# State-space stage: running sums spread over the partitions by DMA through DRAM in place of selector products, and C.B read from PSUM

## Chip, cores and metric

The kernel runs on one core of one Trainium2 chip. The time is device time of one execution, in microseconds (us); the runs shown are compared by their median. A profile is one further execution, seen by the hardware profiler. "Page" below is the page that the profile makes of that execution.

## What is computed

Two transformer-like blocks in a row, in float32, on 512 tokens of 1024 features. The first block holds a state-space mixer (Mamba-2) and a sliding-window attention; the second one a differential attention, a sparse attention and two convolutional feed-forward layers. The change concerns the state-space mixer alone. Cut to what matters there (32 heads of 64 features in 8 groups of 4 heads, chunks of 128 tokens, 4 chunks):

```python
a_cs = jnp.cumsum(a, axis=-1)                        # a = dt * A; within a chunk, per head
seg = a_cs[..., :, None] - a_cs[..., None, :]
decay = jnp.exp(jnp.where(causal, seg, -jnp.inf))
cb = jnp.einsum('bclgn,bcsgn->bcgls', Cc, Bc)
y_diag = jnp.einsum('bcgrls,bcsgrp->bclgrp', cb[:, :, :, None] * decay, x)
...
y_off = jnp.einsum('bclgn,bcgrpn,bcgrl->bclgrp', Cc, h_in, jnp.exp(a_cs))
return (y_diag + y_off).reshape(b, L, SSM_HEADS, P)
```

So each head needs its running sum a_cs twice: as a difference between any two tokens of a chunk (the decay), and exponentiated per token (for what comes in from earlier chunks).

## The kernel before

Everything is kept as features on partitions by tokens along the free dimension. Products of weights with activations are exact to float32 by splitting both into a high and a low part (wH, wL, hH, hL): three TensorE products of 128 by 128 by 512 for each block of 128 weights rows, 24 for one output block, all recorded under line 365 (`gemm`). The weights come as a stream: a load of 512 KB (raw, four buffers) on SP's queue, a copy on ScalarE that makes wH (L319), a subtraction on VectorE that makes wL (L321); wH and wL have four buffers each. One such chunk feeds the 24 products of one output block.

The stage (`mamba`) computes the time steps and the running sums first. `pacs` holds the sums with tokens on partitions, `acs` (L616 to L618) holds them with heads on rows 0 to 31 and, as a rest that a float32r copy leaves, on rows 32 to 63. Then it loops over the 8 groups. For a group g:

- Four projections (two x blocks, B, C), each followed by a short convolution on VectorE (u, L626; xc, L631) and Silu on ScalarE (L633); two more projections for the gate z (L638, L639).
- Transposes of x (ps_t, L650) make xdt and xde on VectorE; transposes of B (L661) make bt on ScalarE (L662).
- C.B of the four chunks goes to a PSUM bank (L666) and is copied by ScalarE to cbs (L669).
- The states h after each chunk (L674, L679 to L682).
- For each pair of heads (i = 0, 1): for each head r a product selr x acs (L692) sets the head's running sums on all 128 partitions of a bank pa; four Relu on ScalarE (L696, one per chunk, with pacs as bias) and an Exp (L698) make the decay m; GpSimd masks it (L699); VectorE multiplies it with cbs (L701). Eight products yd of m with xdt follow (L705). A product sel2 x acs (L711) does the same for the pair's exponentials e (L714). Three products yf of the states with C (L716). VectorE puts them together into y (L720 to L724).

ps_s, the PSUM banks of yd, yf and pa, has 2 buffers, ps_t 2, ps_g (projections) 3, ps_o 1.

The code names no order between engines: a scheduler in the building layer puts each engine's instructions in a row, and so lets the projection products of group g + 1 run among the small products at the end of group g. Each engine, and SP's DMA queue, runs its row in order. After groups 3 and 5 a part of the output product is done (L735 to L740).

Of the kernel before, what the change touches and what calls it, by code (L numbers as in the profile page):

```python
# [9 lines left out]
F32 = mybir.dt.float32  # L10
F32R = mybir.dt.float32r
# [3 lines left out]
ALU = mybir.AluOpType  # L15

P = 128
# [21 lines left out]
W3 = 0  # L39
ALL_STAGES = ("mamba", "swa", "da", "ffn0", "dsa", "ffn1", "final")  # L40
# [5 lines left out]
# ---------------------------------------------------------------- host layout  # L46
# [17 lines left out]
def _stage_blocks(stage, a):  # L64
    """The stage's weights as [128, 128] blocks in the order in which the program takes them."""
# [148 lines left out]
# ---------------------------------------------------------------- the program  # L214
class _Kernel:
    """The stages, all on features by tokens: x is the residual stream, hH + hL the normed operand without its
    1 / rms (exactly, as two float32r parts), rb and rt 1 / rms on all partitions and per token."""
# [24 lines left out]
    # ---- shared state  # L242
# [60 lines left out]
    # ---- the weight stream  # L303
# [5 lines left out]
    def wchunk(self, pool=None, name=""):  # L309
        """Emits the next group of 8 blocks: load, high and low parts."""  # L310
# [14 lines left out]
    def wget(self, n=1):  # L325
        """High and low parts of the stream's next n blocks."""
        c, r = divmod(self.wi, 8)
        assert r + n <= 8
        if r == 0:
            while self.wemit <= min(c + 1, self.ws.shape[0] - 1):  # L330
                self.wchunk()
            self.wchunks.pop(c - 6, None)
        H, L = self.wchunks[c]
        self.wi += n
        return H[:, r * P:(r + n) * P], L[:, r * P:(r + n) * P]
# [4 lines left out]
    # ---- PSUM and products of features by tokens  # L340
# [9 lines left out]
    def gemm(self, w, H, L, cuts, M=P, spread=False, late=False):  # L350
        """The product, cut by tokens: (PSUM view, first token, tokens). spread takes score banks as well; late
        leaves what needs L to the end."""
# [19 lines left out]
    # ---- norms  # L372
    def square_in(self, src, k, c0, cn, eng=None, acc=None):
        """acc += src ** 2."""
# [9 lines left out]
    def parts_of_x(self, k, g, t0, t1, T):  # L384
        """High and low parts of x * g of feature block k, tokens t0 to t1 of the residual."""
# [13 lines left out]
    def next_h(self, k, g, t0, t1, T):  # L399
        """What the next layer takes of feature block k."""  # L400
# [4 lines left out]
    def rsqrt(self, dst, v, rows=P):  # L405
        """dst = v ** -0.5 of small SBUF operands: a power, then a Newton step."""
# [17 lines left out]
    def token_sums(self, T, half=None, acc=None):  # L424
        """Sums of acc over the features, a column per token tile."""
# [11 lines left out]
    def spread_rows(self, src, T, half=None):  # L437
        """PSUM views [128, tokens] with src[t] of a token-on-partition column set on all partitions."""
# [16 lines left out]
    def norm_end(self, T, half=None):  # L455
        """rt and rb of the tokens from acc."""
# [8 lines left out]
    def post_stats(self, half, acc, rg=None):  # L465
        """PSUM view with 1 / rms of (rg * ys) on all partitions, for half of the first block's tokens; acc holds
        the squares of ys."""
# [18 lines left out]
    def post_update(self, half, rp, ys, xs, g_post, g_next, T_next):  # L486
        """x = xs + g_post * rp * ys, and the next layer's operand."""
# [24 lines left out]
    def out_halves(self, pool, H, L, ys, xs, g_post, g_next, T_next, acc, rg=None, part=True):  # L512
        """The last part of a first-block layer's output product, half of the tokens at a time, and the norm; ys
        holds what comes before if part."""
        nc = self.nc
        n = len(H)
        # all of the weights stay for the second half: the first ones in the ring, the others in the pool
# [28 lines left out]
    # ---- the state-space mixer  # L546
    def mamba(self, g_next):
        nc, T = self.nc, SEQ
        tc = self.tc
        with ExitStack() as ctx:  # L550
# [7 lines left out]
            selr = cp.tile([64, 32], F32R, name="selr")  # L558
            nc.vector.tensor_tensor(selr, self.ident[:64, :32], self.ident[:64, 32:64], ALU.add)
# [3 lines left out]
            # time steps, 128 tokens x (4 chunks x 32 heads)  # L563
# [29 lines left out]
            # decays  # L593
# [22 lines left out]
            acs = cp.tile([64, T], F32R, name="acs")  # L616
            nc.scalar.activation(acs[:32], ps[:32, :T], AF.Copy)
            nc.vector.tensor_tensor(acs[32:64], ps[:32, :T], acs[:32].bitcast(F32), ALU.subtract)  # L618

            for g in range(GROUPS):  # L620
                xc, sz = [], []
                for i, b in enumerate((2 * g, 2 * g + 1, 16 + g, 24 + g)):
# [19 lines left out]
                # tokens on partitions: x * dt, x * dt * decay to the chunk's end, B  # L642
# [20 lines left out]
                # C B per chunk, keys on partitions  # L663
                cb = self.ps("t")
# [3 lines left out]
                cbs = wp.tile([P, T], F32, name="cbs", bufs=1)  # L668
                nc.scalar.activation(cbs, cb[:, :T], AF.Copy)  # L669
                # states after each chunk  # L670
# [13 lines left out]
                # outputs, two heads (a block of features) at a time  # L684
                for i in range(2):
                    yd = self.ps("s")
                    yf = self.ps("s")
                    ms = []
                    for r in range(2):
                        hd = 4 * g + 2 * i + r  # L690
                        pa = self.ps("s")
                        nc.tensor.matmul(pa[:, :T], selr[:, hd:hd + 1].to_broadcast([64, P]), acs, start=True,  # L692
                                         stop=True)
                        m = wp.tile([P, T], F32, name="m", bufs=2)
                        for c in range(4):
                            nc.scalar.activation(m[:, P * c:P * c + P], pa[:, P * c:P * c + P], AF.Relu,  # L696
                                                 bias=pacs[:, 32 * c + hd:32 * c + hd + 1], scale=-1.0)
# [763 lines left out]
```

## Time and profile before

| | |
|---|---|
| median of 3 runs | 2216.05 us (2211.14 to 2216.69) |
| span of the profiled execution | 2209.3 us; its own time is not given apart from the span, which is 6.75 us under the median of the runs |
| instructions | 38252 |
| TensorE busy, share of span | 2141.4 us, 97% |
| VectorE busy | 1542.3 us, 70% |
| ScalarE busy | 1001.8 us, 45% |
| GpSimd busy | 252.1 us, 11% |
| DMA, mean over the span | 79 GB/s |
| the state-space stage's loop | about 45 to 440 us |

How to read it: PE is TensorE's products, PEld its weight loads (which run beside products), DVE VectorE, ACT ScalarE, POOL GpSimd, SPq the DMA queue of SyncE. "L365" is a line of the kernel. An arrow such as ps_g<-hH,wH names the tile written and the tiles read. Products are pipelined, so a product's listed duration is longer than the distance between two starts. In a list of waits, "A <- B" says that A's engine stood idle until B was done.

### The profile page before, as it was taken

To read this page: it belongs to the slowest core of one execution; us is meant where nothing else is said; L and a number is where in the kernel's file an instruction comes from. 1 tells how busy PE (TensorE), PEld (TensorE's weight loads), DVE (VectorE), ACT (ScalarE), POOL (GpSimd) and SP (SyncE) were. 2 spreads that over 40 slices of the span, in tenths; PEclk is the share of its full clock that TensorE was granted. 3 is DMA by queue.
4 is the path that set the end of the run, shared out by engine and by line. 5 is a ranking of instruction groups with operands and counts; after the bars stand their busy time and mean duration, and the time that the engine had idled before them with its cause. 6 is when DMAs were issued, how large, how long until landed. Compare 5 with 4: busy or idle time off the path is not lost.

```text
span 2209.3 us, 38252 instructions
## 1 busy us (share of the span) xinstructions
PE 2141.4 (97%) x15108; PEld 1908.7 (86%) x15108; DVE 1542.3 (70%) x3336; ACT 1001.8 (45%) x1939; POOL 252.1 (11%) x380
## 2 busy tenths in 40 slices
PE   8999999999998999999999999999999999999998
PEld 6777777787777888888999999979788889999997
DVE  7776676778766677886664466489888866645653
ACT  6565544545775454454342243343444434423431
POOL 0111010142102211212000000110110110000001
PEclk9999999999999999999999999999999999999999
DMA  5222222233221212222232322321321223323321
GB/s 182 67 58 77 76 77 77 70 107 96 58 67 57 89 58 51 76 68 67 77 96 86 96 87 86 90 65 58 87 59 49 69 77 87 95 87 96 96 86 48
DMA packets 52306, 174.49 MB, mean 79 GB/s; under 512 B 7328, under 2 KB 9376, under 8 KB 52128
## 3 DMA queue, kind: packets, MB, share of 16 engines
q1 hardware_dynamic: 50976, 171.01, 26.2%
q8 instruction: 119, 1.95, 0.4%
q10 hardware_dynamic: 1152, 1.05, 0.1%
q14 instruction: 59, 0.48, 0.1%
HBM read 160.23 MB, written 2.10 MB: 73 GB/s over the span
## 4 chain that ended last, share of the span: by engine, by line
PE 54%; DVE 9%; issue 2%; ACT 1%; POOL 1%; POOLq 0%; DVEq 0%; ACTq 0%
PE ps_g L365 29%; PE ps_s L365 13%; PE ps_o L1243 2%; PE ps_s L1007 2%; PE ps_o L1133 2%; PE ps_g L790 1%; DVE wL L321 1%; DVE sel L1345 1%; PE ps_t L1035 1%; DVE m L1344 1%; PE ps_s L972 1%; POOL rs_r L411 1%; PE ps_t L1032 1%; DVE sel L1325 1%; DVE hL L396 1%
## 5 line engine op out<-in xcount | busy, mean ns | idle before, releaser
L365 PE MATMUL ps_g<-hH,wL 128*128 128x256 f32 (+3 forms) x1912 | 614.0, 321 | 0.4 <-DVE wL L321 0.4
L365 PE MATMUL ps_g<-hL,wH 128*128 128x256 f32 (+3 forms) x1912 | 609.7, 320 | 2.7 <-DVE hL L396 2.7
L365 PE MATMUL ps_g<-hH,wH 128*128 128x256 f32 (+3 forms) x1912 | 608.2, 318 | 0.4 <-ACT hH L391 0.3
L319 ACT ACTIVATE wH<-raw 128x1024 fp32r<-128x1024 f32 x294 | 310.8, 1058 | 396.4 <-PE ps_g L365 228.4
L321 DVE TENSOR_TENSOR wL<-raw,wH 128x1024 fp32r<-128x1024 f32 x294 | 364.3, 1241 | 146.2 <-ACT wH L319 145.8
L365 PEld LDWEIGHTS ps_g<-hH,wH 128*128 128x128 f32 x1912 | 362.2, 189 | 28.5 <-issue 4.5
L365 PEld LDWEIGHTS ps_g<-hL,wH 128*128 128x128 f32 x1912 | 361.4, 189 | 29.3 <-DVE hL L396 4.3
L365 PEld LDWEIGHTS ps_g<-hH,wL 128*128 128x128 f32 x1912 | 362.4, 190 | 26.9 <-issue 5.5
L365 PE MATMUL ps_s<-hH,wH 128*128 128x256 f32 (+5 forms) x608 | 178.3, 294 | 7.9 <-ACT hH L391 7.9
L365 PE MATMUL ps_s<-hH,wL 128*128 128x256 f32 (+5 forms) x608 | 178.2, 293 | 0.6 <-DVE wL L321 0.6
L365 PE MATMUL ps_s<-hL,wH 128*128 128x256 f32 (+5 forms) x608 | 177.2, 294 | 0.8 <-DVE hL L396 0.4
L382 POOL TENSOR_TENSOR acc<-acc,sq 128x512 f32<-128x512 f32 (+3 forms) x62 | 75.5, 1217 | 554.5 <-ACT sq L381 552.9
L1380 DVE SCALAR_TENSOR_TENSOR c<-u,prm,c 128x528 f32<-128x528 f32 (+1 forms) x176 | 132.9, 755 | 3.5 <-ACT c L1377 1.8
L772 POOL TENSOR_TENSOR rt<-rt,S 128x272 f32<-128x272 f32 (+3 forms) x80 | 81.1, 1016 | 414.9 <-DVE rt L770 325.5
L365 PEld LDWEIGHTS ps_s<-hH,wH 128*128 128x128 f32 (+2 forms) x608 | 115.6, 190 | 10.2 <-ACT hH L391 9.0
L365 PEld LDWEIGHTS ps_s<-hL,wH 128*128 128x128 f32 (+2 forms) x608 | 114.6, 189 | 5.0 <-DVE hL L396 3.7
L365 PEld LDWEIGHTS ps_s<-hH,wL 128*128 128x128 f32 (+2 forms) x608 | 116.0, 191 | 3.3 <-DVE wL L321 1.4
L365 PE MATMUL ps_g<-aH,wH 128*128 128x256 f32 (+1 forms) x418 | 118.1, 283 | 0.3
L365 PE MATMUL ps_g<-aL,wH 128*128 128x256 f32 (+1 forms) x418 | 118.1, 282 | 0.0
L365 PE MATMUL ps_g<-aH,wL 128*128 128x256 f32 (+1 forms) x418 | 118.1, 282 | 0.0
L797 ACT ACTIVATE aH<-sg 128x528 fp32r<-128x528 f32 (+1 forms) x44 | 28.1, 639 | 126.8 <-DVE sg L1385 126.8
L365 PE MATMUL ps_s<-aH,wH 128*128 128x256 f32 (+1 forms) x286 | 80.4, 281 | 0.4 <-ACT aH L797 0.4
(498 smaller groups left out, 4556.1 us busy)
## 6 DMA issues: line engine op xcount, KB each, us to landing
raw<-in_ws_dram SPq DMA_DIRECT2D x294, 512.0 KB, 3.6
k<-k SPq DMA_DIRECT2D x32, 264.0 KB, 3.6
x<-in_xT_dram SPq DMA_DIRECT2D x8, 256.0 KB, 4.8
xo<-in_xT_dram SPq DMA_DIRECT2D x8, 256.0 KB, 5.4
k<-k SPq DMA_DIRECT2D x4, 256.0 KB, 7.5
out_dram<-x SPq DMA_DIRECT2D x8, 128.0 KB, 1.7
out_dram<-x ACTq DMA_DIRECT2D x8, 128.0 KB, 1.7
C<-in_tab_dram SPq DMA_DIRECT2D x2, 264.0 KB, 5.1
```

The costliest lines, as they stand in the source:

```text
L319: nc.scalar.activation(H, self.raw, AF.Copy)
L321: nc.vector.tensor_tensor(L, self.raw, H.bitcast(F32), ALU.subtract)
L365: nc.tensor.matmul(ps[:M, :cn], w[k][a][:, :M], b[k][:, c0:c0 + cn], start=i == 0, stop=i == 3 * n - 1)
L382: (eng or nc.gpsimd).tensor_tensor(acc, acc, s[:, :cn], ALU.add)
L396: self.nc.vector.scalar_tensor_tensor(L, self.x[k][:, t0:t1], self.col(g, k), H.bitcast(F32), ALU.mult, ALU.subtract)
L411: nc.gpsimd.tensor_tensor(r, v, self.mhalf[:rows, :n], ALU.pow)
L772: nc.gpsimd.tensor_tensor(t, t, S[:, cc], ALU.mult)
L797: nc.scalar.activation(H[:, cols], src, AF.Copy)
L1007: nc.tensor.matmul(ps, q[:, r, t0 - q0:e - q0], k[:, r, k0:k1], start=n == 0, stop=n == 1 and not last)
L1133: nc.tensor.matmul(dst, aT[j], vs[j][:ENDS[j] - STARTS[j], hc], start=j == 0, stop=j == i)
L1243: nc.tensor.matmul(dst, vs[j][:ENDS[j] - STARTS[j], hc], pT[r][j], start=j == 0, stop=j == i, skip_group_check=True)
L1380: nc.vector.scalar_tensor_tensor(c[:, lo:], u[:, t + lo:t + T2], self.col(fw, 3 * b + t), c[:, lo:], ALU.mult, ALU.add)
```

## The change

The running sums are no longer split in two and multiplied with selectors. `acs` stays float32 on 32 partitions and is stored in a DRAM tile (`acs_d`); its exponential is made once for all heads and stored as well (`eas_d`). A function `decay(hd)` loads one head's row of `acs_d` with a DMA that repeats the row on 128 partitions into a tile m (6 buffers), and does Relu, Exp and mask in place; it is called for the four heads at the head of the group's loop. e is loaded in the same way from `eas_d`, two halves of 64 partitions. C.B goes to the bank ps_o instead of ps_t, and VectorE's product of m reads it there; the copy cbs is gone, and the four products of a group stand right behind C.B.

```diff
+MB = 6
...
-            selr = cp.tile([64, 32], F32R, name="selr")
-            nc.vector.tensor_tensor(selr, self.ident[:64, :32], self.ident[:64, 32:64], ALU.add)
+            dram = self.pool(ctx, "md", 1, space=bass.MemoryType.DRAM)
...
-            acs = cp.tile([64, T], F32R, name="acs")
-            nc.scalar.activation(acs[:32], ps[:32, :T], AF.Copy)
-            nc.vector.tensor_tensor(acs[32:64], ps[:32, :T], acs[:32].bitcast(F32), ALU.subtract)
+            acs = wp.tile([32, T], F32, name="acs", bufs=1)
+            nc.scalar.activation(acs, ps[:32, :T], AF.Copy)
+            acs_d = dram.tile([32, T], F32, name="acs_d")
+            nc.sync.dma_start(acs_d, acs)
+            eas = wp.tile([32, T], F32, name="eas", bufs=1)
+            nc.scalar.activation(eas, ps[:32, :T], AF.Exp)
+            eas_d = dram.tile([32, T], F32, name="eas_d")
+            nc.sync.dma_start(eas_d, eas)
+
+            def decay(hd):
+
+                m = wp.tile([P, T], F32, name="m", bufs=MB)
+                nc.sync.dma_start(m, acs_d[hd:hd + 1, :].to_broadcast([P, T]))
+                for c in range(4):
+                    nc.scalar.activation(m[:, P * c:P * c + P], m[:, P * c:P * c + P], AF.Relu,
+                                         bias=pacs[:, 32 * c + hd:32 * c + hd + 1], scale=-1.0)
+                nc.scalar.activation(m, m, AF.Exp, scale=-1.0)
+                nc.gpsimd.affine_select(m, m, pattern=[[0, 4], [1, P]], compare_op=ALU.is_ge, fill=0.0,
+                                        base=0, channel_multiplier=-1)
+                return m
...
+                ms = [decay(4 * g + r) for r in range(4)]
...
-                cb = self.ps("t")
+                cb = self.ps("o")
...
-                cbs = wp.tile([P, T], F32, name="cbs", bufs=1)
-                nc.scalar.activation(cbs, cb[:, :T], AF.Copy)
-                # states after each chunk
+                for m in ms:
+                    nc.vector.tensor_tensor(m, m, cb[:, :T], ALU.mult)
...
-                    ms = []
-                    for r in range(2):
-                        hd = 4 * g + 2 * i + r
-                        pa = self.ps("s")
-                        nc.tensor.matmul(pa[:, :T], selr[:, hd:hd + 1].to_broadcast([64, P]), acs, start=True,
-                                         stop=True)
...
-                        nc.vector.tensor_tensor(m, m, cbs, ALU.mult)
-                        ms.append(m)
...
-                                             ms[r][:, P * c:P * c + P], start=True, stop=True)
+                                             ms[2 * i + r][:, P * c:P * c + P], start=True, stop=True)
...
-                    pa = self.ps("s")
-                    sel2 = wp.tile([64, 2, 64], F32R, name="sel2")
-                    nc.vector.tensor_copy(sel2, selr.bitcast(F32)[:, hd:hd + 2, None].to_broadcast([64, 2, 64]))
-                    nc.tensor.matmul(pa[:, :3 * P], sel2.rearrange("k a b -> k (a b)"), acs[:, P:], start=True,
-                                     stop=True)
                     e = wp.tile([P, 3 * P], F32, name="e")
-                    nc.scalar.activation(e, pa[:, :3 * P], AF.Exp)
+                    for r in range(2):
+                        nc.sync.dma_start(e[64 * r:64 * r + 64],
+                                          eas_d[hd + r:hd + r + 1, P:].to_broadcast([64, 3 * P]))
```

Lines after the change stand one further down up to the stage (L365 becomes L366) and some twenty further down inside it. The scheduler's rows move at three places.

TensorE at the end of group 2 (the third group), before: the rows from the first pair's yf (h is the state) to the second pair's selector products. Rows of L365 are the projection of group 3.

```order
L365 MATMUL ps_g<-hH_85,wL 128x512
L716 MATMUL ps_s<-xc_1184,h_1289 128x128
L716 MATMUL ps_s<-xc_1184,h_1293 128x128
L716 MATMUL ps_s<-xc_1184,h_1298 128x128
L365 MATMUL ps_g<-hL_93,wH 128x512
L705 MATMUL ps_s<-m,xdt 64x128 x7
L692 MATMUL ps_s<-acs,selr 128x512
L365 MATMUL ps_g<-hH_86,wH 128x512
L365 MATMUL ps_g<-hH_86,wL 128x512
L365 MATMUL ps_g<-hL_94,wH 128x512
L365 MATMUL ps_g<-hH_87,wH 128x512
L692 MATMUL ps_s<-acs,selr 128x512
```

The same engine and group after, from the state sums (L693) over the first pair's yd to the second pair's:

```order
L693 MATMUL ps_t<-xde,bt 128x256 x2
L709 MATMUL ps_s<-m,xdt 64x128
L366 MATMUL ps_g<-hL_90,wH 128x512
L709 MATMUL ps_s<-m,xdt 64x128 x7
L366 MATMUL ps_g<-hH_83,wH 128x512
L366 MATMUL ps_g<-hH_83,wL 128x512
L366 MATMUL ps_g<-hL_91,wH 128x512
L366 MATMUL ps_g<-hH_84,wH 128x512
L693 MATMUL ps_t<-xde,bt 128x256
L717 MATMUL ps_s<-xc_1197,h_1304 128x128
L709 MATMUL ps_s<-m,xdt 64x128 x8
```

The second pair's yd moved up to the first state product, eight in a row; the selector products are gone; and in the whole row of a group other products break into the projection eight times, where they did so eleven times.

ScalarE at the end of group 2, before: from the first Relu of m to the second pair's.

```order
L696 ACTIVATE m<-ps_s,pacs 128x128 x5
L662 ACTIVATE bt<-ps_t 128x384
L698 ACT_TABLE_LOAD
L698 ACTIVATE m<-m 128x512
L669 ACTIVATE cbs<-ps_t 128x512
L696 ACTIVATE m<-ps_s,pacs 128x128 x3
L698 ACTIVATE m<-m 128x512
L714 ACTIVATE e<-ps_s 128x384
L696 ACTIVATE m<-ps_s,pacs 128x128 x4
L698 ACTIVATE m<-m 128x512
```

After, at the same place; m here belongs to group 3, sq and yH to group 2, xc_1438 to group 3:

```order
L681 ACTIVATE bt<-ps_t 128x384
L631 ACTIVATE m<-m,pacs 128x128 x5
L633 ACT_TABLE_LOAD
L633 ACTIVATE m<-m 128x512
L631 ACTIVATE m<-m,pacs 128x128 x4
L633 ACTIVATE m<-m 128x512
L382 ACTIVATE sq<-y 128x512
L730 ACTIVATE yH<-y,prm 128x512
L647 ACTIVATE xc_1438<-u,prm 128x512
L320 ACTIVATE wH<-raw 128x1024
L631 ACTIVATE m<-m,pacs 128x128 x4
L633 ACTIVATE m<-m 128x512
```

The decay of a group moved into the end of the group before it, and bt stands ahead of it. In the first group all four m stand ahead of bt, with z's Silu between the third and the fourth.

SP's queue before is one row of 65 raw loads through the stage; after, in groups 2 to 4, it reads:

```order
L307 DMA raw<-in_ws_dram 128x1024 x4
L629 DMA m<-acs_d 128x512 x3
L307 DMA raw<-in_ws_dram 128x1024
L629 DMA m<-acs_d 128x512
L714 DMA e<-eas_d 64x384 x4
L307 DMA raw<-in_ws_dram 128x1024 x5
L629 DMA m<-acs_d 128x512 x3
```

The loads of m and e came in between the weight loads, and every raw load behind one of them leaves after it.

## Rows read from the trace of the kernel before

**Rows 1.** Stretches: us, busy of each engine (instructions), clock, DMA share, GB/s.

```profile
45.00:440.00 395.00, 390.97 (x1898) 300.31 (x1897) 285.04 (x400) 215.63 (x378) 45.76 (x75) 1.00 0.25 74
...
143.47:188.42 44.95, 44.50 (x221) 34.14 (x220) 34.56 (x49) 26.04 (x46) 5.84 (x10) 1.00 0.24 72
```

**Rows 2.** Waits, 45 to 440 us: who for whom, us in total, times, longest.

```profile
ACT wH L319 <- PE ps_g L365: 50.2, 25, 5.1
...
PEld ps_s L705 <- DVE m L701: 9.0, 20, 0.7
...
PE ps_s L705 <- DVE m L701: 4.0, 14, 0.6
```

**Rows 3.** Waits of SP's DMA queue, 40 to 460 us.

```profile
SPq L306 <- DVE wL L321: 388.1, 57, 18.2
```

**Rows 4.** Timeline of TensorE in group 2: start us, us, instruction, count.

```profile
144.44 0.72 PE L692 MATMUL ps_s<-acs,selr 64*128 64x512 f32 x2
145.09 0.51 PE L365 MATMUL ps_g<-hH,wH 128*128 128x512 f32 x1
...
151.20 0.43 PE L711 MATMUL ps_s<-acs,sel 64*128 64x384 f32 x1
151.56 0.50 PE L365 MATMUL ps_g<-hL,wH 128*128 128x512 f32 x1
...
153.35 1.09 PE L705 MATMUL ps_s<-m,xdt 128*64 128x128 f32 x14
154.37 0.50 PE L692 MATMUL ps_s<-acs,selr 64*128 64x512 f32 x1
154.80 0.50 PE L365 MATMUL ps_g<-hH,wH 128*128 128x512 f32 x1
...
155.60 0.39 PE L365 MATMUL ps_g<-hH,wH 128*128 128x512 f32 x1
155.91 0.50 PE L692 MATMUL ps_s<-acs,selr 64*128 64x512 f32 x1
...
156.68 0.39 PE L365 MATMUL ps_g<-hL,wH 128*128 128x512 f32 x1
156.91 0.39 PE L365 MATMUL ps_g<-hH,wH 128*128 128x512 f32 x1
```

**Rows 5.** Groups by line and shape, 45 to 440 us: busy us, mean ns.

```profile
L701 DVE TENSOR_TENSOR m<-m,cbs 128x512 f32<-128x512 f32 x32 | 24.6, 769 | 5.6 <-POOL m L699 5.6
...
L638 DVE TENSOR_TENSOR z<-ps_g,rb 128x512 f32<-128x512 f32 x16 | 11.1, 691 | 31.8 <-PE ps_g L365 31.8
...
L714 ACT ACTIVATE e<-ps_s 128x384 f32<-128x384 f32 x16 | 7.9, 492 | 8.5 <-PE ps_s L711 8.4
```

**Rows 6.** DMA issues of the whole span: count, KB each, median us to landing.

```profile
raw<-in_ws_dram SPq DMA_DIRECT2D x294, 512.0 KB, 3.6
...
out_dram<-x SPq DMA_DIRECT2D x8, 128.0 KB, 1.7
...
posi<-in_pos_dram SPq DMA_DIRECT2D x1, 256.0 KB, 5.3
```

**Rows 7.** Timeline of ScalarE in the first group.

```profile
44.26 0.59 ACT L617 ACTIVATE acs<-ps_t 32x512 fp32r<-32x512 f32 x1
...
54.00 1.06 ACT L319 ACTIVATE wH<-raw 128x1024 fp32r<-128x1024 f32 x1 [3.04 <-PE ps_g L365]
...
55.49 1.38 ACT L696 ACTIVATE m<-ps_s,pacs 128x128 f32<-128x128 f32 x5
56.94 0.49 ACT L662 ACTIVATE bt<-ps_t 128x384 f32<-128x384 f32 x1
57.45 1.28 ACT L698 ACT_TABLE_LOAD   x1
58.74 0.63 ACT L698 ACTIVATE m<-m 128x512 f32<-128x512 f32 x1
```

**Rows 8.** Timeline of VectorE in the first group.

```profile
47.15 1.22 DVE L321 TENSOR_TENSOR wL<-raw,wH 128x1024 fp32r<-128x1024 f32 x1
```

More of the change, by code (lines that the diff above doesn't have):

```diff
@@ L687, in mamba @@
                     yf = self.ps("s")
-                    ms = []
-                    for r in range(2):
-                        hd = 4 * g + 2 * i + r
-                        pa = self.ps("s")
-                        nc.tensor.matmul(pa[:, :T], selr[:, hd:hd + 1].to_broadcast([64, P]), acs, start=True,
-                                         stop=True)
[L694 to L697, printed above, removed]
-                        nc.scalar.activation(m, m, AF.Exp, scale=-1.0)
-                        nc.gpsimd.affine_select(m, m, pattern=[[0, 4], [1, P]], compare_op=ALU.is_ge, fill=0.0,
-                                                base=0, channel_multiplier=-1)
-                        nc.vector.tensor_tensor(m, m, cbs, ALU.mult)
-                        ms.append(m)
                     for c in range(4):
```

## Prediction

> **What bounds the kernel now.** The change touches one stage, the state-space mixer, so I read that stage first and not the page's averages: the table of stretches for 45 to 440 us, where its eight groups run, and for one whole group, from one group's first transposes to the next one's [rows 1]. TensorE is busy for 390.97 of 395.00 us there, at a granted clock of 1.00; VectorE has 285 us of work, ScalarE 216, and the DMA engines are a quarter full. One group takes 44.95 us. Then the list of waits of the same stretch [rows 2]: ScalarE's split of the weights (wH) waits for TensorE to give a buffer back, 50.2 us in 25 waits. The suppliers wait for TensorE, so the stage is bound by the number and length of TensorE's instructions. The one wait of TensorE itself that repeats is for m, the masked decay, in front of the yd products: 4.0 us on the product queue in 14 waits, 9.0 us on the weight-load queue in 20, partly the same time. What the change takes from TensorE therefore comes off the time, as long as its new loads and its new order on ScalarE bring m in time.
>
> **What it removes from TensorE.** The selector products: four selr of 512 columns and two sel of 384 in a group. Their price is the shift that each causes in the starts of group 2 [rows 4], not its listed duration, since products overlap. Two projection products in a row start 0.23 apart (156.68 to 156.91). The two selr behind the transposes: 144.44 to 145.09, 0.65. The one behind yd: 154.37 to 154.80, 0.43. The one inside the projection: from 155.60 to 156.68 there are a projection product, selr and another projection product, 1.08 for what takes 0.46 without it: 0.62. Each sel: 151.20 to 151.56, 0.36, twice. Sum 0.65 + 0.43 + 0.62 + 0.72 = 2.42 us a group, **19.4 us** in eight.
>
> The order of TensorE also changes. Before, other work breaks into the projection eleven times in a group; now eight times. One of the three is the single selr, priced above. For the other two: behind selr at 154.80 three projection steps take 0.80 (to 155.60) against 0.69, so a break costs 0.11 on its way out. 2 x 0.11 x 8 = **1.8 us**.
>
> **The waits for m.** m of a group is now made from loads while the group before ends, so that only the product with C.B stands between C.B and yd. Of the waits in [rows 2] at least the 4.0 us on the product queue should go, at most the 9.0 of the weight loads. I take 5, near the lower end, because a new chain (four VectorE products in a row, then the states) may leave some: **5 us**.
>
> **What it adds off TensorE.** VectorE: the four products m x C.B now read PSUM. The nearest rows are z <- ps_g x rb, which reads PSUM at 691 ns, and the old m x cbs, which reads SBUF alone at a mean of 769 [rows 5]: no more per instruction, so nothing. [...]
>
> ScalarE loses e's exponential (16 x 492 ns) [rows 5] and eight copies of C.B, which with 512 columns against e's 384 take at least as long each: together 11.8 us or more. Its order, though, mixes the Exp of m with the Silu of the next group, so 26 table loads stand in the loop where there were 16: 10 x 1.28 [rows 7] = 12.8 us. That about evens out; ScalarE has 179 us idle in the stage. GpSimd's 32 masks stay.
>
> DMA: 32 loads of m (256 KB) and 32 of e (96 KB), 11.5 MB over about 370 us, 31 GB/s on top of 74 [rows 1]; room enough. They go through SP's queue, which is mostly asleep: 388.1 us of it waiting for VectorE to free a raw buffer [rows 3]. What is queued behind a load of m that waits for its buffer are raw loads; what is queued behind a raw load that waits are loads of m and e. A load's time has no row of this program point, but posi is the same form, one 2 KB row of DRAM set on 128 partitions, and it landed in 5.3 us in the company of other loads; a raw load of twice the size takes 3.6 [rows 6]. I take 3.6 to 5.3.
>
> In the steady state that hides. A group's second pair of m buffers comes back with its last yd, which by the new order is some 9 us after the group's first transposes; 5.3 us later the load has landed, and these m are wanted a whole group later. The weights give the cover for ScalarE's stall meanwhile: wH has four buffers, so up to three groups of 24 products (3 x 24 x 0.23 = 17 us) are split ahead; less 1.06 for wH and 1.22 for wL [rows 7, 8], 14 us. e has one buffer, so the second e of a group is loaded after the first is used, and VectorE can stand for 2 or 3 us before e x yf; the bank behind that is asked for by TensorE only in the next group, and VectorE has 28% idle.
>
> **The first group** has no group before it to hide in. The running sums are on SBUF at 44.85 (44.26 + 0.59); a store of 128 KB lands in 1.7 [rows 6], and this is half of that; the raw load ahead of m in SP's queue waits for wL, done at 48.37 [rows 8]. So the first m lands at 52.0 to 53.7. ScalarE had nothing to do from 50.96 (54.00 less 3.04) on [rows 7]. Four Relu at 0.28 (five in 1.38), a table load and Exp: the first Exp starts by 56.1, before it was 58.74. The later ones come at about 1.7 each, but z's Silu cuts in with two more table loads and bt, copied at 56.94 before, now stands behind all four: about 65. TensorE asks for bt behind 32 projection products and the first yd, 7.4 us and 1.1 (32 x 0.23, and the yd row at 153.35, [rows 4]) after what used to be its place, 65.4. So 0 to 2 us are lost, once; I take **1 us**. [...]
>
> **Sum.** 19.4 + 1.8 + 5 - 1 = 25.2 us, 25 for short. The profiled execution spans 2209.3 us, 6.75 below the median of the runs; nothing around the span changes, so I take the difference off the median: 2216.05 - 25 = **2191 us**. The bounds of these terms: all of 9.0 of the waits and no loss in the first group, 30 us, 2186; two more us of instruction gaps as TensorE drops its 64-row switches, 2184; only 4.0 and 2 lost, 23 us, 2193.
>
> **Rivals.** (a) *More*: every wait of TensorE for m goes, and the merged blocks save more than 0.11. For it: m is ready a group ahead. 2184. (b) *A new wait takes the place*: four products of 0.69 in front of the state sums on VectorE push the states 2.8 us later than before, and TensorE, whose order has yf close behind them, stands for half of that: 1.4 x 8 = 11 us, 2203. For it: VectorE is at 72% already (285 of 395 us) and at 77% if the stage shrinks to 370. Against: eight yd and some projection products stand in between. (c) *No change*: the selector products were filling time in which TensorE would have waited for m anyway, so their room fills with waits. Against: [rows 2] shows waits of 4.0 us beside 19.4 of products, and the weights are ready early. 2216. (d) *Slower*: the loads of m. All 128 packets of a load read the same 2 KB of DRAM, and SP runs in order; ScalarE stands in front of each group's Relu until they land, with wH and Silu behind it. It decides from 14 us of landing time on, where the split weights run out; each further us then costs 8, so above some 17 us the kernel is slower than before. At 20 us: 8 x 6 - 25 = +23, 2239. Against: 5.3 for posi [rows 6].
>
> **How the numbers follow.** Forecast (2187 to 2196) 0.60; (a) 0.15; (b) 0.13; (c) 0.07; (d) 0.05. The likeliest gives 2191. The range takes in (a) and (b) with a little room, 2181 to 2205, and leaves (c) and (d) out. What differs by under 0.3%, some 6.6 us, a measurement of this kernel can't tell from no change: faster is the forecast with (a) and (b), 0.88; the same 0.07; slower 0.05.
>
> **What the profile of after would show.** Right: no instruction on acs in TensorE, a group period of some 42 us in place of 44.95, TensorE 98% busy or more in the stage, wH still waiting for TensorE, TensorE's waits for m near nothing. Loads of m that land in under 6 us. Wrong: TensorE waiting for h or m in each group (b); a period still near 45 (c); raw or wH waiting for DMA, ScalarE idle in front of Relu for over 10 us, TensorE waiting for wL (d). A first group that is longer than the others by more than 3 us would show the step on bt wrong.

## Result and profile after

The changed kernel takes **2184.3 us** (median of 4 runs, 2182.8 to 2188.0) against 2214.2 us of the kernel before beside it (2211.1 to 2216.7): a ratio of 0.987, 95% interval 0.986 to 0.988. The profiled execution spans 2183.5 us, 25.8 less than before. The 1600th projection product, which lies just behind the state-space stage, starts 460.7 us after TensorE's first product in the execution before and 432.5 after: 28.2 us come from the stage. The other 2.4 us go the opposite way: TensorE's first product starts 0.7 us later, and what comes behind the 1600th, the same work as before, takes 1.7 us longer. That lies within what single executions differ by (a second execution of the kernel after has 28.5 for the stage, the same first start as before to 0.1 us, and 0.5 us behind).

The stretches of the changed stage answer to [rows 1]; the second one is group 2, from transposes to transposes (columns: us, busy of each engine with instructions, clock, DMA share, GB/s).

```profile
45.00:412.00 367.00, 365.17 (x1850) 293.32 (x1849) 276.15 (x385) 221.22 (x367) 51.24 (x74) 1.00 0.36 111
139.87:181.15 41.28, 41.28 (x214) 33.26 (x213) 34.16 (x47) 27.40 (x45) 6.11 (x10) 1.00 0.37 118
```

A group takes 41.28 us in place of 44.95, and TensorE has no idle time in it at all. The first two groups take 44.14 and 41.53 (43.68 and 41.55 in a second execution). ScalarE has 5.6 us more work than before, the DMA engines move 111 GB/s in place of 74. The waits, 40 to 430 us, answer to [rows 2].

```profile
ACT wH L320 <- PE ps_g L366: 43.6, 16, 10.4
...
ACT m L631 <- DMA m<-acs_d: 39.7, 7, 6.4
...
DVE e L723 <- PE ps_s L717: 9.8, 7, 1.6
...
PE ps_s L709 <- DVE m L688: 0.9, 1, 0.9
PE ps_g L366 <- DVE wL L322: 0.8, 1, 0.8
...
PEld ps_s L709 <- DVE m L688: 4.0, 9, 1.3
PEld ps_t L693 <- ACT bt L681: 2.2, 7, 0.3
```

ScalarE still waits for TensorE to give wH buffers back. New is its wait for the loads of m, seven times, some 6 us each; TensorE has nothing of that. Its product queue waits once for m, 0.9 us, and once for wL, 0.8 us, both in the first group. Its weight loads wait for bt, 0.3 us at a time in seven groups, and still for m, 4.0 us in nine waits where it was 9.0 in twenty. SP's queue (same stretch) answers to [rows 3]: it still waits mostly for wL, and now also for e's buffer (L724) and for m's buffers from yd (L709) and from the products with C.B (L688).

```profile
SPq L307 <- DVE wL L322: 191.1, 49, 14.1
SPq L714 <- DVE y L724: 37.8, 15, 4.9
SPq L629 <- PE ps_s L709: 37.0, 14, 7.3
SPq L629 <- DVE m L688: 36.7, 8, 6.3
```

TensorE in group 2 answers to [rows 4]: no product on acs, and the yd of a pair stand together, but for one projection product in the first pair.

```profile
144.31 0.43 PE L709 MATMUL ps_s<-m,xdt 128*64 128x128 f32 x2
144.67 0.50 PE L366 MATMUL ps_g<-hL,wH 128*128 128x512 f32 x1
145.10 1.09 PE L709 MATMUL ps_s<-m,xdt 128*64 128x128 f32 x14
```

VectorE's product of m, now with C.B in PSUM, and the table loads, 45 to 412 us (busy, mean ns), answer to [rows 5, 7]; the landing times (last column, us) to [rows 6].

```profile
L688 DVE TENSOR_TENSOR m<-m,ps_o 128x512 f32<-128x512 f32 x32 | 20.0, 678 | 3.4 <-POOL m L634 3.4
...
L633 ACT ACT_TABLE_LOAD x13 | 16.7, 1283 | 0.2
L652 ACT ACT_TABLE_LOAD x12 | 15.4, 1283 | 0.2
L658 ACT ACT_TABLE_LOAD x2 | 2.6, 1283 | 0.0
```

```profile
raw<-in_ws_dram SPq DMA_DIRECT2D x294, 512.0 KB, 3.7
...
m<-acs_d SPq DMA_DIRECT2D x32, 256.0 KB, 3.7
e<-eas_d SPq DMA_DIRECT2D x32, 96.0 KB, 2.8
...
acs_d<-acs SPq DMA_DIRECT2D x1, 64.0 KB, 3.7
```

The first group, on SP's queue and on ScalarE (start, us, instruction, idle time before it in brackets), answers to [rows 7].

```profile
45.60 0.42 SPq L620 DMA_DIRECT2D acs_d<-acs  x1
...
49.35 1.76 SPq L629 DMA_DIRECT2D m<-acs_d  x4
```

```profile
54.27 1.58 ACT L631 ACTIVATE m<-m,pacs 128x128 f32<-128x128 f32 x5 [3.24 <-DMA m<-acs_d]
55.87 1.28 ACT L633 ACT_TABLE_LOAD   x1
57.16 0.63 ACT L633 ACTIVATE m<-m 128x512 f32<-128x512 f32 x1
...
65.84 0.47 ACT L681 ACTIVATE bt<-ps_t 128x384 f32<-128x384 f32 x1
...
76.73 2.94 ACT L320 ACTIVATE wH<-raw 128x1024 fp32r<-128x1024 f32 x3
```

The store of the sums takes 3.7 us to land, the loads leave at 49.35, the first one lands 4.9 us later and the first Relu starts at 54.27. bt is copied at 65.84. Then ScalarE works on the m of group 1 too, and the next wH comes at 76.73.

### The profile page after: what moved, and what is told of

It reads as the page before. It is cut to its first block, busy times and chain, and to the rows that moved or that the text cites. A ratio compares the mean times of both kernels' runs of the same rounds, so it can differ in the third digit from the quotient of the medians.

```text
span 2183.5 us, 38225 instructions
## 1 busy us (share of the span) xinstructions
PE 2118.2 (97%) x15060; PEld 1905.7 (87%) x15060; DVE 1533.0 (70%) x3318; ACT 1004.8 (46%) x1925; POOL 261.1 (12%) x380
## 3 DMA queue, kind: packets, MB, share of 16 engines
q10 hardware_dynamic: 1152, 1.05, 0.1%
## 4 chain that ended last, share of the span: by engine, by line
PE 79%; DVE 12%; issue 3%; ACT 2%; POOL 2%; DMA 1%; SPq 0%; POOLq 0%; DVEq 0%; ACTq 0%
PE ps_g L366 49%; PE ps_s L366 14%; PE ps_o L1244 2%; PE ps_s L1008 2%; PE ps_g L791 2%; PE ps_o L1134 2%; DVE wL L322 2%; DVE sel L1346 1%; DVE hL L397 1%; PE ps_t L1036 1%; POOL rs_r L412 1%; DVE m L1345 1%; PE ps_s L709 1%; PE ps_o L931 1%; PE ps_s L973 1%
## 5 line engine op out<-in xcount | busy, mean ns | idle before, releaser
L366 PE MATMUL ps_g<-hL,wH 128*128 128x256 f32 (+3 forms) x1912 | 610.1, 320 | 2.3 <-DVE hL L397 2.3
L366 PE MATMUL ps_g<-hH,wL 128*128 128x256 f32 (+3 forms) x1912 | 609.9, 319 | 1.7 <-DVE wL L322 1.7
L366 PE MATMUL ps_g<-hH,wH 128*128 128x256 f32 (+3 forms) x1912 | 607.4, 318 | 0.5 <-ACT hH L392 0.3
L366 PEld LDWEIGHTS ps_g<-hL,wH 128*128 128x128 f32 x1912 | 361.0, 189 | 29.5 <-issue 4.2
L366 PEld LDWEIGHTS ps_g<-hH,wL 128*128 128x128 f32 x1912 | 361.7, 189 | 27.4 <-issue 3.3
L366 PEld LDWEIGHTS ps_g<-hH,wH 128*128 128x128 f32 x1912 | 361.6, 189 | 26.0 <-issue 3.0
L366 PE MATMUL ps_s<-hH,wH 128*128 128x256 f32 (+5 forms) x608 | 178.2, 293 | 8.6 <-ACT hH L392 8.6
L366 PE MATMUL ps_s<-hH,wL 128*128 128x256 f32 (+5 forms) x608 | 178.2, 293 | 0.6 <-DVE wL L322 0.6
L366 PE MATMUL ps_s<-hL,wH 128*128 128x256 f32 (+5 forms) x608 | 177.7, 295 | 0.9 <-DVE hL L397 0.6
L366 PEld LDWEIGHTS ps_s<-hH,wH 128*128 128x128 f32 (+2 forms) x608 | 115.8, 191 | 10.7 <-ACT hH L392 9.5
L366 PEld LDWEIGHTS ps_s<-hL,wH 128*128 128x128 f32 (+2 forms) x608 | 115.8, 192 | 4.4 <-DVE hL L397 3.2
L366 PEld LDWEIGHTS ps_s<-hH,wL 128*128 128x128 f32 (+2 forms) x608 | 116.3, 191 | 3.0 <-DVE wL L322 1.4
L366 PE MATMUL ps_g<-aH,wH 128*128 128x256 f32 (+1 forms) x418 | 118.5, 284 | 0.3
L366 PE MATMUL ps_g<-aH,wL 128*128 128x256 f32 (+1 forms) x418 | 118.7, 284 | 0.0
L366 PE MATMUL ps_g<-aL,wH 128*128 128x256 f32 (+1 forms) x418 | 118.6, 284 | 0.0
L366 PE MATMUL ps_s<-aH,wH 128*128 128x256 f32 (+1 forms) x286 | 80.5, 282 | 0.4 <-ACT aH L798 0.4
```

The source lines that it names most:

```text
L366: nc.tensor.matmul(ps[:M, :cn], w[k][a][:, :M], b[k][:, c0:c0 + cn], start=i == 0, stop=i == 3 * n - 1)
```

## Experiments

A group's period is the time from the start of its eight transposes of x to that of the next group's. "After" is the changed kernel, and each edit is made to it, but for the one that says otherwise. A ratio is to the kernel before, measured beside the run. In three of the kernels (only m by DMA, C.B copied, seven buffers of m) acs also takes the space of another tile, to make room. An edit can also change the row that the scheduler writes for TensorE.

**The selector products alone.** Six products a group are put back, unread, with the shapes of the old ones, on other operands.

```diff
+                    for r in range(2):
+                        pa = self.ps("s")
+                        nc.tensor.matmul(pa[:, :T], self.hH[1][:64, r:r + 1].to_broadcast([64, P]),
+                                         self.hH[0][:64, :T], start=True, stop=True)
...
+                    pa = self.ps("s")
+                    nc.tensor.matmul(pa[:, :3 * P], self.hH[1][:64, :P], self.hH[0][:64, P:T], start=True,
+                                     stop=True)
```

> The changed kernel with the six selector products of each group kept as products that nobody reads (same sizes, on the operand hH; the computation is the changed kernel's). Theory (the gain is TensorE's own time in these products and the breaks they make): period back to 44.0 to 44.9 us, time 2205 to 2212. Rival (most of the gain was TensorE no longer waiting for m): period under 42.5, time under 2194.

Measured: 2206.97 us (before 2214.2; ratio 0.997, 0.996 to 0.998), period 44.57. So 3.29 us of the 3.67 a group go with these products; all the rest of the change is worth 0.38 a group. In the whole time the products cost 22.7 us and not eight times 3.29, mostly since the first group of this kernel (45.41) loses only 0.8 against its later ones, where the first group of after loses 2.9.

**The same products over 128 rows.** The only edit to that kernel: `[:64, ...]` becomes `[:, ...]` in the operands. The order of TensorE's row is the same, instruction by instruction.

> The six unread products of the kernel that keeps them, in the same places of TensorE's row, but over 128 rows of the operands in place of 64. Theory (their price is mostly that of switching to 64 rows and back, which the neighbours pay too): the group period falls from 44.57 to 42.6 to 43.2, since four products of 512 columns and two of 384 cost 1.3 us if nothing is switched, 2194 to 2199. Rival (it is the breaks and the products alone, whatever their rows): the period stays at 44.6, 2207.

Measured: 2198.2 us (ratio 0.9945, 0.993 to 0.996), period 43.29. The two kernels show one stretch of group 2 each, first with 64 rows, then with 128.

```profile
151.77 0.47 PE L366 MATMUL ps_g<-hH,wL 128*128 128x512 f32 x1
152.17 0.50 PE L709 MATMUL ps_s<-hH,hH 64*128 64x512 f32 x1
152.60 0.50 PE L366 MATMUL ps_g<-hL,wH 128*128 128x512 f32 x1
153.03 0.49 PE L709 MATMUL ps_s<-hH,hH 64*128 64x512 f32 x1
153.45 0.50 PE L366 MATMUL ps_g<-hH,wH 128*128 128x512 f32 x1
153.88 1.09 PE L713 MATMUL ps_s<-m,xdt 128*64 128x128 f32 x14
```

```profile
149.26 0.48 PE L366 MATMUL ps_g<-hH,wL 128*128 128x512 f32 x1
149.58 0.40 PE L709 MATMUL ps_s<-hH,hH 128*128 128x512 f32 x1
149.81 0.39 PE L366 MATMUL ps_g<-hL,wH 128*128 128x512 f32 x1
150.04 0.49 PE L709 MATMUL ps_s<-hH,hH 128*128 128x512 f32 x1
150.37 0.40 PE L366 MATMUL ps_g<-hH,wH 128*128 128x512 f32 x1
150.69 1.09 PE L713 MATMUL ps_s<-m,xdt 128*64 128x128 f32 x14
```

The same five products take 2.11 us (151.77 to 153.88) with 64 rows and 1.43 (149.26 to 150.69) with 128, and the projection product between the two costs 0.43 in the one and 0.23 in the other: what the 64 rows cost here, 0.68 us, lies half in the neighbours (0.39 in the slots of the three projection products, 0.29 in those of the two others). Of the 3.29 us, 1.28 are the 64 rows and 2.01 the six products themselves with the breaks that they make.

**Only m by DMA.** e is made by sel2 x acs and an Exp again, as in the kernel before.

```diff
+                    pa = self.ps("s")
+                    sel2 = wp.tile([64, 2, 64], F32R, name="sel2")
+                    nc.vector.tensor_copy(sel2, selr.bitcast(F32)[:, hd:hd + 2, None].to_broadcast([64, 2, 64]))
+                    nc.tensor.matmul(pa[:, :3 * P], sel2.rearrange("k a b -> k (a b)"), acr[:, P:], start=True,
+                                     stop=True)
...
+                    nc.scalar.activation(e, pa[:, :3 * P], AF.Exp)
```

> The changed kernel with e made as before, by the product sel x acs and an Exp on ScalarE; only m comes by DMA. Theory: two products of 0.36 us and their breaks come back, 0.7 to 0.9 us a group, period 42.0 to 42.2, time 2190 to 2192. Rival (the loads of e hold VectorE up and cost time of their own): period at or under 41.3, time at or under 2184.

Measured: 2196.9 us (ratio 0.992, 0.991 to 0.994), period 42.63: longer than either side expected. With two sel products a group is 1.35 us longer, 0.68 for each, nearly twice the 0.36 between a sel's start and the next start [rows 4]. Not all of it need be theirs: in TensorE's row two yf now split the second pair's yd, which stand in one run of sixteen in after, and the yd of a group take 2.76 us in place of 2.40. The first group is longer too (47.0), and that is part of the 12 us.

**C.B copied to SBUF again.**

```diff
-                cb = self.ps("o")
+                cb = self.ps("t")
...
+                cbs = wp.tile([P, T], F32, name="cbs", bufs=1)
+                nc.scalar.activation(cbs, cb[:, :T], AF.Copy)
                 for m in ms:
-                    nc.vector.tensor_tensor(m, m, cb[:, :T], ALU.mult)
+                    nc.vector.tensor_tensor(m, m, cbs, ALU.mult)
```

> The changed kernel with one part undone: C.B goes to ps_t and is copied by ScalarE to cbs in SBUF, and VectorE's four products read that copy. Theory (a PSUM source costs VectorE nothing that can be seen, the copy only stands in the way): products of m near 0.69 us as in the changed kernel, group period 41.3 to 42.0 us against 41.27, time 2184 to 2190. [...]

Measured: 2190.6 us (ratio 0.9895, 0.988 to 0.991), period 41.74. VectorE's products of this kernel, 45 to 420 us, TensorE's wait in the first group, and the stretch in which that wait ends:

```profile
L690 DVE TENSOR_TENSOR m<-m,cbs 128x512 f32<-128x512 f32 x32 | 19.9, 684 | 3.7 <-ACT cbs L688 3.7
```

```profile
PE ps_g L366 <- DVE wL L322: 3.2, 1, 3.2
```

```profile
88.00:92.00 4.00, 3.04 (x9) 2.43 (x10) 3.97 (x5) 2.94 (x8) 0.10 (x1) 0.73 0.34 131
```

684 ns with C.B in SBUF, 678 with C.B in PSUM: the read from PSUM shows no cost. A group is 0.46 us longer, though TensorE waits for nothing in it: the row has another order, with the yd of both pairs split (2.76 us for 2.40), so the 0.46 is not to be put down to the copy alone, and the copy and the change of bank were not tried apart. In the first group the wait for wL grows from 0.8 to 3.2 us; the granted clock of this stretch is 0.73.

**Longer loads of m.** Each load of m is made twice, or four times, one behind the other's landing; the last one alone counts.

```diff
-                nc.sync.dma_start(m, acs_d[hd:hd + 1, :].to_broadcast([P, T]))
+                for n in range(2):
+                    nc.sync.dma_start(m, acs_d[hd:hd + 1, :].to_broadcast([P, T]))
```

> Each m is loaded twice, the second load behind the first one's landing, so a decay row is there 7.4 us after its issue in place of 3.7, and SP's queue stands 3.7 us for each of the 32 loads. The cover theory (ScalarE may stand up to 14 us in a group before the split weights run out): group periods stay at 41.3, only the first group, which has no cover, loses 3 to 8 us: 2187 to 2192. Rival (landing counts at once, about 3.7 us a group): periods 45, 2214.

Measured: 2190.8 us (ratio 0.991, 0.989 to 0.992); the periods are 42.96, 42.51, 41.85, 65.54, 41.28, 67.51 and 41.28, where after has 44.14, 41.53, 41.28, 63.65, 41.27, 63.63 and 41.27 (the fourth and the sixth hold a part of the output product). So some groups lose up to 3.9 us, others nothing. The time lies in the range expected, but not for the reason given: the first group, which was to lose 3 to 8 us, is shorter than in after, and later ones lose. One of the losses, on VectorE and on TensorE:

```profile
289.21 1.22 DVE L322 TENSOR_TENSOR wL<-raw,wH 128x1024 fp32r<-128x1024 f32 x1 [2.94 <-ACT wH L320]
```

```profile
292.37 0.52 PE L681 MATMUL ps_t<-ident,xc 128*128 128x128 f32 x3 [2.16 <-DVE xde L676]
```

VectorE stands for a wH that ScalarE made late, and xde, which empties the bank that TensorE wants next, stands behind that wL in VectorE's row. The scheduler also wrote other rows for this kernel, so that not all of it need be the landing time.

> Each m is loaded four times in series: 14.8 us from issue to the last landing, and SP stands 3 x 3.7 = 11 us for each, 44 us a group, more than the period of 41.3. Cover theory: the edge of 14 us is passed, the loads become the bound, periods 45 to 50, first group 10 to 20 us longer, in all 2215 to 2260, slower than the kernel before. Rival (the loads hide whatever they take): 41.3, 2185.

Measured: 2213.5 us (ratio 1.000, 0.9995 to 1.001), periods 47.35, 46.73, 48.49, 69.54, 42.76, 64.41 and 45.03: the gain is gone, but the kernel is not slower than the one before, as the theory had it (2215 to 2260). Waits of SP and of TensorE (40 to 430 us), and one wait of TensorE in group 2 with what stands before it on ScalarE, and the stretches around it:

```profile
SPq L630 <- DMA m<-acs_d: 118.3, 82, 3.9
```

```profile
PE ps_o L686 <- ACT xc L653: 8.9, 3, 4.2
...
PE ps_s L710 <- DVE m L689: 2.7, 1, 2.7
```

```profile
143.36 0.69 ACT L632 ACTIVATE m<-m,pacs 128x128 f32<-128x128 f32 x2 [3.33 <-DMA m<-acs_d]
...
151.90 0.61 ACT L653 ACTIVATE xc<-xc 128x512 f32<-128x512 f32 x1
```

```profile
152.56 1.65 PE L686 MATMUL ps_o<-xc,xc 128*128 128x128 f32 x6 [3.52 <-ACT xc L653]
```

```profile
150.00:154.00 4.00, 1.44 (x6) 1.44 (x7) 2.85 (x6) 3.97 (x8) 0.68 (x2) 0.69 0.01 2
154.00:158.00 4.00, 4.00 (x14) 3.29 (x13) 2.48 (x4) 3.97 (x6) 0.64 (x1) 0.50 0.00 0
```

The largest wait is not for split weights but for the Silu of B and C (xc), which stands in ScalarE's row behind the Relu of a late m: 3.33 us for the load, then m, table loads and z, and only then xc. And a wait of 3.52 us costs more than itself: in the 4 us behind it, with TensorE busy all the time, the granted clock is 0.50 (behind the wait of 2.7 for m in the first group, at 0.50 from 72 to 76 us, projection products start 0.42 to 0.43 apart, where they start 0.23 apart at 1.00). SP itself stands 118 us for landings, so that raw loads wait behind loads of m too; the runs don't divide the loss between that and ScalarE's row. On TensorE's side they do: its products wait 19.5 us in the stage, where those of after wait 1.7, and its mean granted clock from 45 to 440 us is 0.97, where the stage of after has 1.00. By an estimate from these rows that is 18 us of waits and 12 of clock (0.03 x 395), for 29 us lost.

**The first group's m behind bt.** The call of `decay` for group 0 stands behind the copy of bt.

```diff
-                ms = [decay(4 * g + r) for r in range(4)]
+                ms = [decay(4 * g + r) for r in range(4)] if g else None
...
+                ms = ms or [decay(4 * g + r) for r in range(4)]
```

> The changed kernel with the decay of the first group alone written behind its copy of bt, so that z's Silu and bt stand ahead of most of it on ScalarE. Theory A (the late bt and the table loads ahead of it cost the first group its gain): first period from 44.14 to 42.5 us or less, time 2182 to 2183. Theory B (it is the landing of the first m and then wH, made late behind the m of the second group, with TensorE waiting for wL): first period stays at 43.7 to 44.5, time within 1 us of 2184.

Measured: 2182.2 us (ratio 0.986, 0.984 to 0.987), first periods 43.47 and 40.57. TensorE's wait for m goes from 0.9 to 0.2, the one of 0.8 for wL stays. The first period lies between what the two theories asked for, a little under B's. By the two periods 1.2 to 1.6 us come back, which the medians alone would not tell from nothing, and 0.7 of it is that the second group is shorter than a steady one, in a row of another order: each pair's yd stand in one run of sixteen.

```profile
101.80 1.09 PE L710 MATMUL ps_s<-m,xdt 128*64 128x128 f32 x16
...
104.36 1.09 PE L710 MATMUL ps_s<-m,xdt 128*64 128x128 f32 x16
```

The yd of this group take 2.05 us, start to start; in a steady group of after, where one projection product splits the first pair's, 2.40.

**Buffers of m.** `MB = 4`, then `MB = 7`.

> m has 4 buffers in place of 6, so no load of a group's m leaves before the yd of the group before has given its buffer back. Cover theory: that is still nearly a group ahead of its use, periods stay at 41.3; the first group may even gain 1 to 2 us, since wH no longer stands behind the m of group 1: 2182 to 2186. Rival (six buffers are what keeps m's landing off the path): TensorE waits for m in each group, 1 to 3 us, 2192 to 2208.

> m has 7 buffers (acs shares the space of another tile to make room). Cover theory: ScalarE's wait for m's landing, about 6 us a group now, shrinks, the period stays at 41.3: 2183 to 2186. Rival (the wait is on the path): 2175 to 2181.

Measured: 2183.1 and 2184.0 us (ratios 0.987 both, 0.986 to 0.989), periods of 41.2 to 41.3 from the second group on in both (63.6 with a part of the output product). With four buffers the wait for wL in the first group is gone, and the one for m is 1.2. So two buffers fewer lose nothing, and ScalarE's wait for m's landing (41.9 us with four, 38.1 with seven) is not on the path.

**Both edits, beside the kernel after.**

> The decay of the first group behind bt, and four buffers for m, so that neither bt nor the wH of the first group stands behind the m of group 1. Theory: both waits of TensorE in the first group go, first period 42 in place of 44.1 and the others 41.3, 2 to 3 us less than the kernel after: 2181 to 2183. Rival (they only change places): 2184.

> The kernel after, unchanged, beside the one with both edits, so that the two stand against the same runs of the kernel before: 2184.

Measured: 2181.5 us (ratio 0.986, 0.985 to 0.988) and 2183.0 (0.987, 0.985 to 0.988). With both edits the wait for wL is gone and that for m is 1.9: one wait took the other's place, and the first period is 43.93, where the theory asked for 42 and after has 43.68 in the execution beside it. The 1.5 us between the two kernels lie within their intervals, and the fault of the first group is not mended by this.

## The prediction, step by step

**What bounds the stage: right.** TensorE is busy without a gap in a steady group (41.28 of 41.28 us), and what was taken from its row came off the time. The reading of [rows 1, 2] that ScalarE and VectorE wait for TensorE held for a stage 7% shorter.

**The selector products: the right cause, too small.** The step took 2.42 us a group; with the products kept, the period shows 3.29, so 26 us in eight groups for 19.4. The term failed where it took five of the six by the distance to the next start. To see it, give each product of group 2 the time from its start to the next one's start, and add up by kind (us):

| | before | after | 64-row kept | 128-row kept |
|---|---|---|---|---|
| projection (144) | 35.66 | 34.25 | 34.63 | 34.06 |
| selector or kept products (6) | 2.24 | - | 2.24 | 1.65 |
| yd (32) | 2.73 | 2.40 | 2.76 | 2.76 |
| states (6) | 1.05 | 1.49 | 1.49 | 1.49 |
| yf (12) | 1.17 | 1.18 | 1.28 | 1.37 |
| transposes, C.B | 2.10 | 1.96 | 2.16 | 1.95 |
| group | 44.95 | 41.28 | 44.56 | 43.28 |

The kept products' own slots are 2.24, as before; the other 1.05 lie in the slots of their neighbours. Where the step looked at both sides, at the one selr inside the projection (1.08 for what takes 0.46), it got 0.62, and the pair measured above costs about that: 2.11 less 0.23 for each of the three projection products is 1.42, 0.71 each with the breaks. The 64 rows themselves had been named, as a bound of the sum ("as TensorE drops its 64-row switches"), at 2 us, which no row had given; the two kept kernels, whose rows have the same order, put them at 1.28 a group, 10 us in eight. One caution: the kept products stand in other places of the row than the old ones did, so that the split between 3.29 and the rest is that of this kernel. Of the 1.05, 0.36 lie in yd, whose second pair is split by two yf in both kept kernels and stands in one run in after; C.B copied, with no product kept, has 2.76 as well. Counted as order, that leaves 2.93 for the products, 23 us in eight groups: still more than 19.4.

**Two breaks fewer (1.8) and the waits for m (5): too large together.** With the selector products kept, the rest of the change is worth 0.38 us a group, 3 us in eight, not 6.8 (0.74 and 6 with yd's 0.36 counted here). The waits of TensorE for m went from 4.0 to 0.9 us on the product queue and from 9.0 to 4.0 on the weight-load queue: less than the lower bound of the step, by which all of the 4.0 was to go. But the states cost 0.44 us a group more than before: they now stand right behind the copy of bt, and the weight loads wait for it, 2.2 us in seven groups. That is the chain that the step feared, through bt rather than through VectorE's four products; how much of the 0.44 is that wait and how much the place was not taken apart.

**PSUM for C.B: right.** 678 ns from PSUM, 684 from SBUF in the same stage. The kernel that copies C.B to SBUF first took 6 us longer (2190.6 for 2184.3), through TensorE's order and the first group's wait, and not through VectorE's reads.

**ScalarE and its table loads: right in size.** 27 table loads in the stage for 26 foreseen; its busy time rose by 5.6 us where it was to even out, off the path. Exp starts 0.01 us behind the load (55.87 and 1.28, 57.16).

**The loads of m and e: right, the cover not.** m lands in 3.7 us (median) for 3.6 to 5.3 assumed; the first six, issued close together, took 4.9 to 6.2. VectorE's wait before e x yf is for yf (L717, 9.8 us in seven waits), not for e. But the point from which loads would hurt was set at 14 us, by the split weights alone; with a load of some 8 us (two in series) single groups already lose 2 to 4, and with four in series the gain is all gone. ScalarE's row holds Silu besides wH behind the late Relu, VectorE's row holds xde behind the late wL, and TensorE's clock is low at the waits of 3.2 and 3.5 us shown above (0.73 and 0.69) and behind them (0.84 and 0.50). Rival (d) was a real one, with a nearer edge than its text said; at 3.7 us it isn't reached.

**The first group: wrong.** It was to lose 0 to 2 us, and 1 was taken. Against 41.28 the first two groups lose 2.86 and 0.25, together 3.1 (2.7 in the second execution). bt came at 65.84 as foreseen ("about 65"), and TensorE doesn't wait for it. Two steps failed. The store of the sums was taken as half of a store of 128 KB that lands in 1.7 us; it took 3.7, so that the loads left at 49.35 in place of 48.37, and the first m came at 54.27 in place of 52.0 to 53.7. TensorE waited 0.9 for m; in the second execution, where m came at 53.26, it waited 0.5. And ScalarE went on from the m of group 0 to those of group 1, so that the next wH came at 76.73, and TensorE had to wait for its wL (with four buffers, which keep the m of group 1 back, this wait is gone):

```profile
82.03 0.50 PE L366 MATMUL ps_g<-hH,wL 128*128 128x512 f32 x1 [0.84 <-DVE wL L322]
```

That is the cover of [rows 7, 8] used up, in the one group where it was not looked for. The rest is a third fault, which no step looked at. By the time from start to start, the first group's 2.86 are 1.74 of these two waits, 0.44 in the other slots of the projection, and 0.68 of another order in TensorE's row: the yd and yf of the two pairs are mixed, 4.65 us for both kinds in place of 3.58, and the states take 1.10 in place of 1.49. In the kernel before the first group had the order of all the others. With four buffers, where the wait for wL is gone and this order stays, the first period is still 43.29; with the decay of the first group behind bt the order is another one again, with 43.47 and 43.93. The sign that the prediction named, a first group longer by more than 3 us, did not show (2.9 and 2.4), and it was set for bt, which was not the fault.

**The sum.** 25 was forecast and 28.2 found in the stage: 26.3 from the selector products, 3.0 from order and waits, less 3.1 in the first two groups, makes 26.2. The other 2 us are the group with the second part of the output product (68.22 before, 63.63 after, 0.9 more than the others gained) and, as much again, the eighth group with what follows it. The two faults of the prediction, 7 us too little and 6 too much, nearly met (4 and 3 with yd's share counted as order); the total is nearer than its terms, and that is luck. By the medians the gain is 29.9 us, and the median of the kernel before, with a fourth run, is 1.8 us under the 2216.05 that the forecast started from. So 2184.3 lies in the range, but not in the forecast's 2187 to 2196: it meets the figure of rival (a), 2184, whose reasons (all waits for m gone, dearer breaks) the runs don't bear out. The same figure stands as a bound with the 64-row products, and that is the reason which they show. In rival (b), 2191 and 11 make 2202, not 2203.

## What to carry to other kernels

On a stage that TensorE fills, price an instruction by what the whole row loses, its neighbours' slots included: read a stretch with it and one without it between the same two kinds of products, and not the distance to the next start. A value that several partitions need came by DMA at no cost here in a steady group (TensorE busy for all of its 41.28 us), where its load was asked for a whole group ahead; look then for the first step, which has no step before it, and count there the store, the load, all that the waiting engine has queued, and the order that the scheduler gives to that step. When you work out how late a supplier may be, take the shortest of all the things queued behind it, not the one with the most buffers.

## What the runs showed of the hardware

The six products over 64 rows that were kept among products over 128 cost 1.28 us a group more than the same six over 128 rows, about 0.2 us each, half of it in the slots of the other products (their own six fell from 2.24 to 1.65). VectorE's product of 128 by 512 float32 with one operand in PSUM took 678 ns, with both in SBUF 684. A store of 64 KB from 32 partitions to DRAM took 3.7 us to land, longer than the 1.7 of 128 KB to the output; a load of one 2 KB row onto 128 partitions took 3.7 (median of 32, 3.1 to 6.5), as long as a weight load of twice the bytes. After a single wait of TensorE of 3.5 us the granted clock stood at 0.50 for 4 us, although the engine was busy again; after one of 2.2 us (two loads in series, the wait that ends at 292.37) it was 0.62 from 294 to 298 us; behind the 0.9 us waits of the kernel after it stayed at 1.00.
